# A two-phase mixer layer: adaLN columns loaded and summed together, an 18-strip first projection, later v, and another layout at the seam

## The chip, the core and the metric

The kernel runs on one core of one Trainium2 chip. Five engines work side by side, each through its own queue in order: TensorE (PE in the profile, with its weight loads as PEld), VectorE (DVE), ScalarE (ACT), GpSimd (POOL) and SyncE (SP), which here issues most of the DMA transfers. The metric is the device time of one execution in microseconds (us), as the median of several runs; it was 2493.97 us before (2492.70 to 2501.88 in 3 runs).

## What is computed

One layer of a hybrid model on a sequence of 2048 tokens of width 1024, all in float32: a mixer (a gated short convolution beside a gated delta rule with 4 heads of 128, in chunks of 64 tokens), a feed-forward part, and a last norm. Norms are adaptive: their shift and scale come from a condition vector c.

```python
def adaln(x, gain, shift, scale):
    return rms_norm(x, gain) * (1 + scale[:, None, :]) + shift[:, None, :]

mod = silu(c) @ w_ada + b_ada                      # 6 x 1024 columns
shift_m, scale_m, gate_m, shift_f, scale_f, gate_f = split(mod, 6)
h = adaln(x, g_norm_mix, shift_m, scale_m)
gate_b, gate_c, h_conv, q, k, v, z, a, bt = split(h @ w_in)
ya = group_norm(gate_b * conv3(gate_c * h_conv))
q, k, v = silu(conv4(concat(q, k, v)))
yb = rms_norm(chunked_gated_delta_rule(l2(q), l2(k), v, g(a), sigmoid(bt))) * silu(z)
x = x + gate_m * (concat(ya, yb) @ w_out)
h = adaln(x, g_norm_ffn, shift_f, scale_f)
gt, up = split(h @ w_gate_up)
x = x + gate_f * ((silu(gt) * up) @ w_down)
out = adaln(x, g_norm_final, shift_o, scale_o)
```

## The kernel before

The sequence is cut into four blocks of 512 tokens. A float32 product is made of three passes over rounded operands (high x high, high x low, low x high); `split_w` (L383 to L388) makes the high half of a weight strip on ACT (L385) and the low half on DVE (L387), or on the engine that `lo_engines` names.

**Opening and first phase.** Blocks 0 and 1 are projected together, by a fast scheme with seven products for each pair of strips (`PAIRS`), whose operands are sums of halves of the two blocks (A11, A12, S1 to S4, A22). Its first operands need x of block 0, normed and transposed, and the scale and shift columns of adaLN, `Gm` and `Sm`. These columns are sums over the 1024 rows of `w_ada`, in three parts of 3, 3 and 2 column groups of 128 (`PARTS`). For part 0, `sums_pe` (L842) sums the scale on PE with the condition column as the moving operand, and `sums_on` (L850) the shift on DVE. For parts 1 and 2 (`late`, `more_rows`, L1058) the scale is summed by DVE and the shift by ACT (multiply) and POOL (add). A sum over DVE or POOL is then added across partitions by PE (`col_sums`, L478). Each transfer is 128 rows of one half's columns, and all of them go round through sixteen places in four tiles, `kd`, `vt`, `zs` and `S3l` (`ada_slots`, L815). All are issued by SP, in the order of the program: x of block 0, the columns, the first four weight strips, the columns of parts 1 and 2, then the small constants, x of block 1 and further strips. `later_sums` (L1099) then norms, transposes and scales block 1 and builds S1 to S4 (L1109 to L1112), and splits them into halves (L1123, L1124). In this opening the framework's scheduler sets the order on each engine.

**Second phase.** From `early.close()` on, the order on each engine is set by a planner (`Clock`): it gives each instruction a cost and a time, places steps of chains between dense matmuls when their inputs are due, and pins that order. Four stages follow (`STAGES`, L410), one for each block whose delta rule is computed. Stage b projects some strips of block 2 or 3 (`dense_strip`, one strip of 128 columns of `w_in` is 24 matmuls), then computes `output(b)`, which multiplies the block's ya and yb with `w_out`. The order of strips is k, q, v, z (four each), then gc, hc, gb four times. While strips run, block b's chains run as side work: the decay, Gram matrices, an inverse of the triangular matrices step by step on DVE (L1449, L1451) with a turn through DRAM, the levels of the inverse (L1490 to L1533), v by `v_chain` (a load, a transposition on PE at L1335, a product at L1578), then the chunk chain (L1600 to L1629) and its outputs `ym` (L1654), which `output` waits for. A chain says how long after its inputs' planned end it wants its next step: `yield v, sk` stands for 0.3 us. `cv` is a tile with four buffers, for convolution, v and the output. Dense strips and outputs take their PSUM banks from one pool of four (`dense_ps`), chains from another of four (`misc_ps`).

**The seam.** After output 3 the mixer's tiles are given up and the feed-forward part begins (`first_sums`, `prep_weights`, `run`). Its pool `fp` starts at the same address as the mixer's pool `la`, which holds only the four `cv` tiles. A tile in the new pool waits for the old tiles under it. `prep_weights` builds its first tile there, `T`, at L1883.

Of the kernel before, what the change touches and what calls it, by code (L numbers as in the profile page):

```python
# [12 lines left out]
F32 = mybir.dt.float32  # L13
# [7 lines left out]
P = 128  # L21
# [189 lines left out]
def layer_kernel(ctx, tc, x, c, w_ada, b_ada, w_ada_final, b_ada_final, g_norm_mix, g_norm_ffn, g_norm_final,  # L211
# [198 lines left out]
    STAGES = (2, 0, 14), (2, 14, 28), (3, 0, 12), (3, 12, 28)  # L410
# [356 lines left out]
    with ExitStack() as actx:  # L767
# [31 lines left out]
        raw_a, raw_d, raw_s1 = (rb.tile([P, 4, BLK], F32, name=n) for n in ("A22h", "A22l", "S4h"))  # L799
        raw_c = rb.tile([P, 4, BLK], F32, name="S4l")  # L800
# [14 lines left out]
        def ada_slots():  # L815
            while True:
                for p, n in ((ra, "kd"), (ra, "vt"), (ra, "zs"), (rb, "S3l")):
                    t = p.tile([P, 4, BLK], F32, name=n)
                    for i in range(4):
                        yield t[:, i]  # L820
        slots = ada_slots()

        PARTS = range(3), range(3, 6), range(6, KD)

        def ada_raw(c0, ks):
            c0, n = c0 + ks[0] * P, len(ks) * P
            for k in range(KD):
                raw = next(slots)[:, :n]
                nc.sync.dma_start(raw, w_ada[k * P:(k + 1) * P, c0:c0 + n])
                yield k, raw  # L830
# [11 lines left out]
        def sums_pe(c0, ks):  # L842
            ps, n = misc_ps(), len(ks)
            for k, raw in ada_raw(c0, ks):
                for j in range(n):
                    mm(ps[:, j:j + 1], raw[:, j * P:(j + 1) * P], cs[:, k:k + 1], start=k + j == 0,
                       stop=k == KD - 1, skip_group_check=True)
            return ps[:, :n]

        def sums_on(eng, raws):  # L850
            acc = cv_tile([P, BLK])[:, :raws[0][1].shape[1]]
            for k, raw in raws:
                if eng is nc.gpsimd:
                    nc.scalar.activation(raw if k else acc, raw, AF.Identity, scale=cs[:, k:k + 1])
                    if k:
                        eng.tensor_add(acc, acc, raw)
                elif k == 0:
                    eng.tensor_scalar_mul(acc, raw, cs[:, 0:1])
                else:
                    eng.scalar_tensor_tensor(acc, raw, cs[:, k:k + 1], acc, op0=ALU.mult, op1=ALU.add)  # L860
            return acc
# [29 lines left out]
        ada_scale(sums_pe(D, PARTS[0]), PARTS[0])  # L891
        x_load(0, 2)
        x_load(0, 3)
        x_norm(0)
        sums = sums_on(nc.vector, list(ada_raw(0, PARTS[0])))
        raws = {p: [load_strip(PAIRS[p][0])] for p in range(EARLY)}
        late = {(c0, n): list(ada_raw(c0, PARTS[n])) for n in (1, 2) for c0 in (D, 0)}
# [4 lines left out]
        ada_shift(col_sums(sums, len(PARTS[0])), PARTS[0])  # L902
# [6 lines left out]
        lo_engines.extend([nc.vector, nc.vector, nc.gpsimd, nc.gpsimd])  # L909
# [187 lines left out]
        nc.scalar.copy(gones_r, gones)  # L1097

# [225 lines left out]
        def start_block(b, prev):  # L1324
# [240 lines left out]
            def v_chain(hs):  # L1565
                while "sk" not in done:
                    yield POLL
                yield from wait("mx", 1)
                if not B.vt:
                    B.vt.append(tile_of([P, CH, NH, P], "vt"))  # L1570
                for h in hs:
                    yield from take("cv", 1)
                    v = cv_tile([P, BLK])
                    nc.sync.dma_start(v, vd[b][h])
                    yield v, sk
                    pv = to_tokens(v)
                    give("cv", 1)
                    nc.vector.tensor_mul(B.vt[0][:, :, h, :], h4(pv), bc(sk[:, h], P))  # L1578
                    done["vt"] += 1
# [142 lines left out]
        def project(w=None):  # L1722
            ps = dense_ps()
            proj(ps, next_w(), *hT)
            return ps
# [103 lines left out]
        for b, (src, s0, s1) in enumerate(STAGES):  # L1829
# [4 lines left out]
            for s in STRIPS[s0:s1]:  # L1834
                dense_strip(src, s, B)
# [16 lines left out]
    fp = fctx.enter_context(tc.tile_pool(name="fp", bufs=1, side="left", reuse_waits="tile"))  # L1852
# [63 lines left out]
    def pair_sums(hf, i, acts):  # L1916
# [487 lines left out]
```

## Time and profile before

| | us |
|---|---|
| median of 3 runs | 2493.97 |
| the profiled execution | 2499.41 |
| its span, first to last instruction | 2497.6 |
| PE busy | 2344.1 |
| DVE busy | 1788.2 |
| ACT busy | 1140.8 |
| POOL busy | 621.3 |

The page gives, for one profiled execution, each engine's busy time, the span in 40 slices, the chain of work that ended last, and groups of instructions by line. Further views of the same trace are used below: PE's waits by what ended them, single instructions in order of time, and the busy time by stretches. In a timeline row the first number is the start in us from the beginning of the span, the second the duration; "x4" says that four were merged, and a bracket names the idle time before the row and what ended it. PE is busy 94% of the span; its granted clock, 1.00 when full, is 0.971 in the mean.

### The profile page before, as it was taken

The numbers are of one execution on the slowest core, as the hardware profiler recorded it, in microseconds if no ns is written. First come the engines' busy times: TensorE is split into PE (matmuls) and PEld (weight loads), VectorE is DVE, ScalarE is ACT, GpSimd is POOL, SyncE is SP. The second block draws the span as 40 slices with busy tenths as digits, with TensorE's granted clock in tenths as the row PEclk, the third lists the DMA queues.
The fourth block names the chain that finished last, engine by engine and source line by source line (L and its number), as shares of the span: only waits on it lengthen the run. The fifth ranks groups of instructions, "written<-read, shape, count | busy, mean of one in ns | idle before, by whom it ended". The sixth has DMA issues, their size and how long they took to land.

```text
span 2497.6 us, 31277 instructions
## 1 busy us (share of the span) xinstructions
PE 2344.1 (94%) x11149; PEld 1933.7 (77%) x11149; DVE 1788.2 (72%) x2699; ACT 1140.8 (46%) x1999; POOL 621.3 (25%) x711
## 2 busy tenths in 40 slices
PE   6899999778999898999999999999999999999997
PEld 5677777667887687887787888878888887887786
DVE  4866988857667697567568655786556569878887
ACT  5756567433653754455643333533333323322345
POOL 3322335144144044211000000000000026344447
PEclk8899999889999899999999999999999999999999
DMA  7736665425454543546477433574333356333334
GB/s 254 233 106 194 186 200 165 134 71 122 127 190 100 167 154 72 126 127 184 137 226 233 134 101 114 173 205 126 100 111 103 103 162 228 121 109 122 138 114 155
DMA packets 399830, 370.05 MB, mean 148 GB/s; under 512 B 41253, under 2 KB 326190, under 8 KB 399418
## 3 DMA queue, kind: packets, MB, share of 16 engines
q1 hardware_dynamic: 390058, 350.91, 45.7%
q0 software_dynamic: 4608, 8.39, 2.3%
q10 hardware_dynamic: 5008, 8.76, 0.9%
q8 instruction: 87, 1.43, 0.2%
q14 instruction: 69, 0.57, 0.1%
HBM read 271.51 MB, written 104.87 MB: 151 GB/s over the span
## 4 chain that ended last, share of the span: by engine, by line
PE 56%; DVE 10%; DMA 8%; issue 8%; POOL 4%; ACT 4%; SPq 0%; ACTq 0%; DVEq 0%; POOLq 0%
PE pd L318 33%; PE pm L318 16%; DVE acc L2258 1%; DMA cv<-v 1%; DVE wlo L387 1%; DMA x<-cv 1%; DMA y<-in_w_ada_final_dram 1%; DMA wraw<-in_w_gate_up_dram 1%; DVE y L467 1%; PE pm L1335 1%; POOL wraw L2187 1%; PE pm L1504 1%; POOL x L1823 1%; PE pm L1496 1%; PE pm L1600 0%
## 5 line engine op out<-in xcount | busy, mean ns | idle before, releaser
L385 ACT CAST whi<-wraw 128x1024 fp32r<-128x1024 f32 x264 | 276.4, 1049 | 348.2 <-PE pd L318 163.9
L387 DVE TENSOR_TENSOR wlo<-wraw,whi 128x1024 fp32r<-128x1024 f32 x262 | 322.8, 1233 | 72.9 <-ACT whi L385 71.7
L318 PE MATMUL pd<-r,whi 128*128 128x512 f32 x1008 | 350.0, 410 | 13.2 <-DVE r L1124 8.3
L318 PEld LDWEIGHTS pd<-r,whi 128*128 128x128 f32 x1008 | 194.5, 193 | 55.2 <-DVE r L1124 10.1
L318 PE MATMUL pd<-r,wlo 128*128 128x512 f32 x504 | 200.8, 398 | 0.0
L2060 POOL TENSOR_TENSOR ht<-y,ht 128x512 fp32r<-128x512 f32 x1 | 1.8, 1838 | 714.1 <-DVE wraw L1885 714.1
L2258 DVE TENSOR_TENSOR acc<-acc,pd 128x512 f32<-128x512 f32 x192 | 127.3, 679 | 25.8 <-PE pd L318 25.0
L2138 ACT CAST xh<-ra 128x640 fp32r<-128x640 f32 (+1 forms) x85 | 60.4, 722 | 183.4 <-PE pm L318 133.8
L2000 DVE TENSOR_TENSOR sg<-sg,pd 128x512 f32<-128x512 f32 x44 | 30.2, 686 | 158.2 <-PE pd L318 158.1
L318 PEld LDWEIGHTS pd<-r,wlo 128*128 128x128 f32 x504 | 97.7, 194 | 16.4
L318 PE MATMUL pd<-whi,ym 128*128 128x512 f32 x256 | 85.3, 406 | 15.8 <-ACT ym L1654 13.9
L2147 POOL TENSOR_TENSOR xl<-ra,xh 128x640 fp32r<-128x640 f32 (+1 forms) x37 | 62.2, 1680 | 146.1 <-ACT xh L2138 135.2
L318 PE MATMUL pd<-A22h,whi 128*128 128x512 f32 x232 | 91.3, 394 | 6.5 <-DVE u L1039 4.0
L2258 DVE TENSOR_TENSOR acc<-acc,pm 128x512 f32<-128x512 f32 x120 | 81.7, 681 | 18.4 <-PE pm L318 17.9
L318 PE MATMUL pd<-S3l,t3h 128*128 128x512 f32 x232 | 91.3, 393 | 0.0
L318 PE MATMUL pd<-A22l,whi 128*128 128x512 f32 x232 | 90.7, 391 | 0.0
L318 PE MATMUL pm<-S4h,whi 128*128 128x512 f32 x232 | 90.6, 390 | 0.2 <-ACT u L1036 0.2
L318 PE MATMUL pm<-S4l,whi 128*128 128x512 f32 x232 | 90.7, 391 | 0.0
L318 PE MATMUL pd<-A22h,wlo 128*128 128x512 f32 x232 | 90.6, 390 | 0.0
L318 PE MATMUL pm<-S4h,wlo 128*128 128x512 f32 x232 | 90.4, 390 | 0.0
L2187 POOL TENSOR_TENSOR wraw<-wraw 128x512 f32<-128x512 f32 x40 | 70.2, 1777 | 48.8 <-DMA wraw<-in_w_down_dram 42.6
L318 PE MATMUL pd<-S2h,whi 128*128 128x512 f32 x176 | 69.6, 395 | 11.9 <-ACT whi L385 11.1
(539 smaller groups left out, 6803.6 us busy)
## 6 DMA issues: line engine op xcount, KB each, us to landing
wraw<-in_w_gate_up_dram SPq DMA_DIRECT2D x88, 512.0 KB, 4.1
wraw<-in_w_in_dram SPq DMA_DIRECT2D x86, 512.0 KB, 5.0
ra<-act SPq DMA_DIRECT2D x80, 448.0 KB, 3.7
act<-S SPq DMA_DIRECT2D x80, 256.0 KB, 3.5
act<-act SPq DMA_DIRECT2D x68, 256.0 KB, 2.2
y<-in_w_ada_dram SPq DMA_DIRECT2D x32, 512.0 KB, 4.5
wraw<-in_w_out_dram SPq DMA_DIRECT2D x32, 512.0 KB, 5.0
wraw<-in_w_down_dram SPq DMA_DIRECT2D x22, 512.0 KB, 3.6
```

What stands on the lines that cost most here:

```text
L318: mm(*args, **kw)
L385: nc.scalar.copy(hi, raw)
L387: (lo_engines.popleft() if lo_engines else nc.vector).tensor_sub(lo, raw, hi.bitcast(F32))
L467: nc.vector.scalar_tensor_tensor(acc, raw, cs[:, k:k + 1], acc, op0=ALU.mult, op1=ALU.add)
L1335: nc.tensor.transpose(ps[:, j * P:(j + 1) * P], src[:, j * P:(j + 1) * P], ident)
L1496: mm(py[:, j * P:(j + 1) * P], Mm[h][:, j, :], T[h][:, j, :], start=True, stop=True)
L1504: mm(pz[:, j * P:(j + 1) * P], Y[h][:, j, :], Xs[h][:, j, :], start=True, stop=True)
L2000: nc.vector.tensor_add(s5[i], s5[i], a[i])
L2138: nc.scalar.copy(hi, raw[:, c0:c1, :])
L2147: eng.tensor_sub(lo, raw, hi.bitcast(F32))
L2187: nc.gpsimd.tensor_mul(r[:, hs], r[:, hs], gate_f[:, hs])
L2258: nc.vector.tensor_add(accs[s, u][:, ns], accs[s, u][:, ns], ps)
```

## The change

It has six edits:

- The first stage projects 18 strips of block 2 in place of 14, the second 10 in place of 14. The cut now falls between hc and gb of the first group.
- Each transfer of adaLN columns brings the shift and the scale columns of 128 rows together (8 transfers a part in place of 16). The parts have places of their own: part 0 in `kd`, `vt`, `zs`, `S3l`; part 1 in `S4h`, `S4l`, `kd`, `vt`; part 2 in `zs`, `S3l`. The tiles `raw_s1` and `raw_c`, which have the places `S4h` and `S4l`, are taken later.
- For part 0, PE sums the scale and DVE the shift as the transfers come; x's third and fourth chunk are loaded behind the fourth transfer. For parts 1 and 2, DVE sums both at once. Nothing of this is left on ACT and POOL, and the first four strips' low halves are all made by DVE.
- `v_chain` places its transposition 3.0 us after the planned landing of v, in place of 0.3.
- The first strip of each stage but the first takes its bank from `misc_ps`.
- The `S` tiles of the feed-forward part lie in a pool of their own, `fs`, ahead of `fp`.

```diff
-    STAGES = (2, 0, 14), (2, 14, 28), (3, 0, 12), (3, 12, 28)
+    STAGES = (2, 0, 18), (2, 18, 28), (3, 0, 12), (3, 12, 28)
...
-        raw_a, raw_d, raw_s1 = (rb.tile([P, 4, BLK], F32, name=n) for n in ("A22h", "A22l", "S4h"))
-        raw_c = rb.tile([P, 4, BLK], F32, name="S4l")
+        raw_a, raw_d = (rb.tile([P, 4, BLK], F32, name=n) for n in ("A22h", "A22l"))
...
+        PLACES = (((ra, "kd"), (ra, "vt"), (ra, "zs"), (rb, "S3l")), ((rb, "S4h"), (rb, "S4l"), (ra, "kd"), (ra, "vt")),
+                  ((ra, "zs"), (rb, "S3l")))
+
+        def ada_raw(part):
+            ks, n_t = PARTS[part], KD // len(PLACES[part])
+            c0, n = ks[0] * P, len(ks) * P
+            rows = w_ada[:, 0:2 * D].rearrange("k (s c) -> k s c", s=2)
+            for q, (pool_, name) in enumerate(PLACES[part]):
+                t = pool_.tile([P, n_t, 2, n], F32, name=name)
+                for i in range(n_t):
+                    k = q * n_t + i
+                    nc.sync.dma_start(t[:, i], rows[k * P:(k + 1) * P, :, c0:c0 + n])
+                    yield k, t[:, i]
...
+        def sums_first():
+            ps, acc, n = misc_ps(), cv_tile([P, BLK])[:, :len(PARTS[0]) * P], len(PARTS[0])
+            for k, raw in ada_raw(0):
                 for j in range(n):
-                    mm(ps[:, j:j + 1], raw[:, j * P:(j + 1) * P], cs[:, k:k + 1], start=k + j == 0,
+                    mm(ps[:, j:j + 1], raw[:, 1, j * P:(j + 1) * P], cs[:, k:k + 1], start=k + j == 0,
                        stop=k == KD - 1, skip_group_check=True)
+                if k == 0:
+                    nc.vector.tensor_scalar_mul(acc, raw[:, 0], cs[:, 0:1])
+                else:
+                    nc.vector.scalar_tensor_tensor(acc, raw[:, 0], cs[:, k:k + 1], acc, op0=ALU.mult, op1=ALU.add)
+                if k == 3:
+                    x_load(0, 2)
+                    x_load(0, 3)
+            return ps[:, :n], acc
+
+        def sums_both(raws):
+            n = raws[0][1].shape[2]
+            acc = temp()[:, :2 * n].rearrange("p (s c) -> p s c", s=2)
             for k, raw in raws:
-                if eng is nc.gpsimd:
-                    nc.scalar.activation(raw if k else acc, raw, AF.Identity, scale=cs[:, k:k + 1])
-                    if k:
-                        eng.tensor_add(acc, acc, raw)
-                elif k == 0:
-                    eng.tensor_scalar_mul(acc, raw, cs[:, 0:1])
+                if k == 0:
+                    nc.vector.tensor_scalar_mul(acc, raw, cs[:, 0:1])
                 else:
-                    eng.scalar_tensor_tensor(acc, raw, cs[:, k:k + 1], acc, op0=ALU.mult, op1=ALU.add)
+                    nc.vector.scalar_tensor_tensor(acc, raw, cs[:, k:k + 1], acc, op0=ALU.mult, op1=ALU.add)
             return acc
...
-        ada_scale(sums_pe(D, PARTS[0]), PARTS[0])
-        x_load(0, 2)
-        x_load(0, 3)
+        ps_g, acc_s = sums_first()
         x_norm(0)
-        sums = sums_on(nc.vector, list(ada_raw(0, PARTS[0])))
         raws = {p: [load_strip(PAIRS[p][0])] for p in range(EARLY)}
-        late = {(c0, n): list(ada_raw(c0, PARTS[n])) for n in (1, 2) for c0 in (D, 0)}
+        late = {n: list(ada_raw(n)) for n in (1, 2)}
...
+        ada_scale(ps_g, PARTS[0])
+        ada_shift(col_sums(acc_s, len(PARTS[0])), PARTS[0])
...
-        lo_engines.extend([nc.vector, nc.vector, nc.gpsimd, nc.gpsimd])
...
-            g, sh = (sums_on(e, late.pop((c0, n))) for e, c0 in ((nc.vector, D), (nc.gpsimd, 0)))
+            acc = sums_both(late.pop(n))
             yield
             n_k = len(PARTS[n])
-            ada_scale(col_sums(g, n_k), PARTS[n])
-            ada_shift(col_sums(sh, n_k), PARTS[n])
+            ada_scale(col_sums(acc[:, 1], n_k), PARTS[n])
+            ada_shift(col_sums(acc[:, 0], n_k), PARTS[n])
...
+        raw_s1, raw_c = (rb.tile([P, 4, BLK], F32, name=n) for n in ("S4h", "S4l"))
...
-                    yield v, sk
+                    yield 3.0, v, sk
...
-        def dense_strip(b, s, B):
+        def dense_strip(b, s, B, bank=dense_ps):
...
-            ps = project()
+            ps = project(bank())
...
-                dense_strip(src, s, B)
+                dense_strip(src, s, B, misc_ps if b and s == STRIPS[s0] else dense_ps)
...
-    fp = fctx.enter_context(tc.tile_pool(name="fp", bufs=1, side="left", reuse_waits="tile"))
+    fs, fp = (fctx.enter_context(tc.tile_pool(name=n, bufs=1, side="left", reuse_waits="tile")) for n in ("fs", "fp"))
...
-            t[o] = fp.tile([P, BLK], F32, name="S", bufs=4)
+            t[o] = fs.tile([P, BLK], F32, name="S", bufs=4)
```

More of the change, by code (lines that the diff above doesn't have):

```diff
@@ L813, in x_norm @@
                     nc.scalar.activation(xts[b][i - 1], xts[b][i - 1], AF.Identity, scale=ss[i - 1])
[L815 to L821, printed above, removed]
-        PARTS = range(3), range(3, 6), range(6, KD)
[L825 to L830, printed above, removed]
+        PARTS = range(3), range(3, 6), range(6, KD)
+        PLACES = (((ra, "kd"), (ra, "vt"), (ra, "zs"), (rb, "S3l")), ((rb, "S4h"), (rb, "S4l"), (ra, "kd"), (ra, "vt")),
[10 more added lines that the diff above has]
+                    yield k, t[:, i]
         def ada_scale(sums, ks):
@@ L901, in layer_kernel @@
             nc.scalar.copy(to[:, k4, :], turned(0, k))
-        ada_shift(col_sums(sums, len(PARTS[0])), PARTS[0])
+        ada_scale(ps_g, PARTS[0])
+        ada_shift(col_sums(acc_s, len(PARTS[0])), PARTS[0])
         H["A11"] = [ra.tile([P, 4, BLK], F32R, name="kq", bufs=2) for _ in range(2)]
@@ L1720, in layer_kernel, with project @@
                 halos[3] = tile_of([P, 12, 3], "halo1"), tile_of([P, 4, 2], "uhalo1")
-        def project(w=None):
-            ps = dense_ps()
+        def project(ps):
             proj(ps, next_w(), *hT)
```

6 lines of the change are left out of this document (removed).

## The prediction

> **What bounds the kernel now.** I read the page first, then the list of PE's waits, then the busy time by stage.
>
> ```profile
> span 2497.6 us, 31277 instructions
> ...
> PE   6899999778999898999999999999999999999997
> ...
> PEclk8899999889999899999999999999999999999999
> ```
>
> Each digit is the busy share of a fortieth of the span (62.4 us), the second row is the granted clock. From slice 20 (1249 us) on PE is full but for the last, so what this change can move lies before: the opening (slices 0 and 1), the delta-rule blocks (slices 6 to 18) and the seam to the feed-forward part behind them, too short to show here.
>
> ```profile
> PE pm L1335 <- DMA cv<-v: 21.4, 9, 4.5
> PE pd L318 <- ACT ym L1654: 13.9, 5, 4.7
> PE pd L318 <- DVE r L1124: 8.3, 3, 5.5
> ```
>
> PE's waits (sum, times, longest): the loads of v, the outputs of the chunk chain, and in the opening the split of S2.
>
> ```profile
> 0.00:28.00 28.00, 17.36 (x88) 16.59 (x88) 6.98 (x17) 15.80 (x26) 4.49 (x16) 1.00 0.95 312
> 28.00:58.00 30.00, 21.90 (x71) 17.16 (x72) 21.91 (x26) 17.64 (x32) 18.81 (x17) 0.72 0.60 190
> 58.00:99.00 41.00, 27.13 (x115) 18.51 (x113) 31.42 (x59) 33.28 (x59) 15.42 (x22) 0.77 0.83 280
> ...
> 475.00:606.00 131.00, 99.52 (x617) 85.24 (x615) 85.88 (x211) 42.03 (x145) 52.29 (x76) 0.88 0.33 91
> 606.00:740.00 134.00, 122.68 (x720) 104.70 (x721) 87.79 (x128) 69.15 (x134) 38.53 (x60) 0.94 0.54 155
> 740.00:804.00 64.00, 62.15 (x314) 50.51 (x314) 51.39 (x122) 29.20 (x84) 27.91 (x32) 0.97 0.47 116
> ```
>
> Columns: stretch, length, busy PE, weight loads, DVE, ACT, POOL, granted clock, DMA share, GB/s. Output of block 0 (475 to 606) leaves PE idle 31.5 us; output of block 1 (740 to 804) leaves 1.9. The opening idles 8.1 (28 to 58) and 13.9 us (58 to 99), at clocks of 0.72 and 0.77: where PE waits, what it does next also runs slower.
>
> **A, the opening.** Before, the scale columns are summed first by PE, the shift columns by DVE; for parts 1 and 2 by DVE and by ACT with POOL. All parts use the same four places, so loads wait for sums. After, each transfer brings both halves (8 per part instead of 16, same bytes), and part 1 lies half in places not used before.
>
> ```profile
> 21.48 2.58 DVE L860 SCALAR_TENSOR_TENSOR cv<-S3l,cs,cv 128x384 f32<-128x384 f32 x4
> ...
> 23.25 2.06 ACT L901 COPY A22l<-pm 128x512 f32<-128x512 f32 x4
> ...
> 28.36 3.12 SPq L829 DMA_DIRECT2D S3l<-in_w_ada_dram  x4
> ...
> 29.39 1.22 PE L318 MATMUL pd<-kq,whi 128*128 128x512 f32 x2 [4.37 <-ACT whi L385]
> ...
> 34.83 5.22 DVE L860 SCALAR_TENSOR_TENSOR cv<-kd,cs,cv 128x384 f32<-128x384 f32 x3
> ...
> 40.07 1.75 SPq L829 DMA_DIRECT2D kd<-in_w_ada_dram  x4
> ...
> 41.00 4.98 POOL L856 TENSOR_TENSOR cv<-cv,S3l 128x384 f32<-128x384 f32 x4
> ...
> 45.28 2.31 PE L481 MATMUL pm<-ones_r,cv 128*128 128x16 f32 x12 [4.36 <-DVE cv L860]
> ...
> 48.75 1.53 DVE L860 SCALAR_TENSOR_TENSOR cv<-vt,cs,cv 128x256 f32<-128x256 f32 x3
> ...
> 51.23 2.29 SPq L805 DMA_DIRECT2D r<-in_x_dram  x4
> ...
> 75.19 0.68 DVE L1109 TENSOR_TENSOR S4h<-S4l,y 128x512 f32<-128x512 f32 x1
> ```
>
> ```profile
> L387 DVE TENSOR_TENSOR wlo<-wraw,whi 128x1024 fp32r<-128x1024 f32 x262 | 322.8, 1233 | 72.9 <-ACT whi L385 71.7
> ```
>
> Timeline rows give start and duration; the last row is a group of the page (busy, mean ns of one). *Part 0*: the scale sum now needs 1.5 MB more to land (5 us at the 312 GB/s of the first row above), the shift sum follows the loads instead of starting behind the scale. No gain: ACT copies until 25.3 us and the first product at 29.39 waits for ACT. *Part 1*: a DVE sum of 384 columns takes 0.645 us alone (2.58/4), but 1.74 (5.22/3) while POOL works. A 768-column one isn't in the trace; between 0.645 and 1.29, I take 1.05, by the step from 256 (0.51) to 384. Eight make about 8 us, two wlo splits taken from POOL add 2.5, the seven slowed sums drop; DVE's total stays about where it was, the sums end near 38 instead of just before 45.28, and PE's first products run until 40.9 (45.28 - 4.36). The wait of 4.36 goes; late next is the scaling by ACT. *Part 2 and the queue*: SP stands from 31.5 to 40.07 and holds every later load. After, nothing waits there: part 2 and then x of block 1 are issued some 15 us sooner. What is loaded up to and with x (2 MB of x, 3.1 for part 0, 2.1 of strips, 3.1 and 2.1 for parts 1 and 2, 2.1 of x) is 14.5 MB, which at 312 GB/s lands near 48 us, so the norm, the transposes and the sums that start with the row at 75.19 come about 10 us earlier, when DVE still has gaps. Of the idle 22 us from 28 to 99, I take **half, -11**; ends -4 (only the wait before L481) and -17 (three quarters). Held at nothing: the later allocation of S4h and S4l (their first other use is behind these sums).
>
> [...]
>
> **B, 18 strips first.** Four strips (z2, z3, gc0, hc0) go ahead of output 0.
>
> ```profile
> 1247.87 5.44 PE pd L318 x24
> ```
>
> A strip is 24 matmuls, 5.44 us by this row of the chain of waits; four are 21.8.
>
> ```profile
> 501.46 2.49 DVE L1490 STREAM_TRANSPOSE lv<-X 128x512 f32<-128x512 f32 x4
> ...
> 502.32 5.81 PE L1496 MATMUL pm<-lv,ym 128*128 128x128 f32 x32 [15.02 <-DVE lv L1490]
> ...
> 559.42 0.59 ACT L1654 CAST ym<-pm 128x512 fp32r<-128x512 f32 x1 [2.08 <-DVE pm L1650]
> ...
> 624.80 2.49 DVE L1490 STREAM_TRANSPOSE lv<-X 128x512 f32<-128x512 f32 x4
> ...
> 723.08 0.59 ACT L1654 CAST ym<-pm 128x512 fp32r<-128x512 f32 x1 [3.48 <-DVE pm L1650]
> ```
>
> Output 0 needs its chain, which ends with the last ym at 560; before it PE idles 15.02 us at once, now covered by these strips. The chain runs on DVE, and four splits (4 x 1.23) and hc0's convolution (about 2.5) are queued among its steps: it ends 0 to 14 us later, I take **+5**. Stage 1 has 21.8 us less to do and loses its v stalls; but output 1 then meets its own chain. By the trace its last ym comes at 723.7, and of the 64 us of output 1 only 42 matmuls (9.5 us) go ahead of it: 723.7 + 54.5 = 778, 26 before 804. If the chain itself advances as PE stalls less, up to 34. I take **-29**. B together **-24** (ends -12 and -34). The cv buffer that hc0 holds over output 0 leaves three of four; I cost it at nothing, since the four evictions of a half are spread over some 9 us of PE work; where they come at once DVE stands behind the store.
>
> **C, later v.** The transposes of v are placed 3.0 instead of 0.3 us after the planned landing.
>
> ```profile
> 814.90 1.09 PE L1335 MATMUL pm<-ck,cv 128*128 128x128 f32 x4 [4.50 <-DMA cv<-v]
> ...
> 824.47 0.66 PE L1335 MATMUL pm<-ck,cv 128*128 128x128 f32 x4 [1.97 <-DMA cv<-v]
> ...
> 1008.93 1.97 PE L1335 MATMUL pm<-ck,cv 128*128 128x128 f32 x8 [3.44 <-DMA cv<-v]
> ...
> 629.65 1.28 DVE L1578 TENSOR_TENSOR vt<-pm,sk 128x512 f32<-128x512 f32 x2
> ...
> 651.85 1.82 DVE L1533 TENSOR_SCALAR X<-pm 64x256 f32<-64x256 f32 x4 [3.95 <-PE pm L1531]
> ```
>
> Blocks 0 and 1 are in B. In blocks 2 and 3 the waits are 9.9; shortened by 2.7 each, 2.5 stay, so **-7** (ends -2 and -12, with the slow clock behind them). Who waits for v: the chunk chain, which also needs the inverse; in block 1 v ends at 630.9, the inverse at 653.7, so a later v is covered by 22 us.
>
> **D, the bank.** The first strip of a stage takes a misc bank, not one that output still empties.
>
> ```profile
> 608.30 0.70 PE L318 MATMUL pd<-r,whi 128*128 128x512 f32 x2 [2.34 <-DVE cv L1822]
> ...
> 998.18 0.70 PE L318 MATMUL pd<-r,whi 128*128 128x512 f32 x2 [2.02 <-DVE cv L1822]
> ```
>
> **-4** (0 to -7). The third stage begins with the narrow product in a misc bank already.
>
> **E, the seam.** The S tiles, used late, get the addresses of the cv tiles; before, T lay there.
>
> ```profile
> 1178.49 0.69 DVE L1884 TENSOR_TENSOR wraw<-wraw 128x512 f32<-128x512 f32 x1
> ...
> 1188.02 0.69 DVE L1883 TENSOR_TENSOR T<-wraw 128x512 f32<-128x512 f32 x1 [8.84 <-DMA x<-cv]
> ...
> 1192.30 0.80 PE L318 MATMUL pd<-S2h,whi 128*128 128x512 f32 x1 [11.05 <-ACT whi L385]
> ```
>
> T waits for the last stores out of cv, and PE for what follows T, 4.28 us later. Without that T starts at 1179.1 and PE at 1183.4: **-9** (-5 to -11). Under T lie the mixer's small tiles then, whose chains have ended; late next is the cast of the strip on ACT, which is in the 4.28.
>
> **The sum**: -11 - 24 - 7 - 4 - 9 = -55. The profiled execution took 2499.41 us (span 2497.6), so 2444; the median of the runs is 2493.97, 5.4 lower, and 2494 - 55 gives 2439. I say 2440.
>
> **Rivals.**
> 1. *Output 1 waits in place of output 0.* For it: the last ym of block 1 comes 98 us after its transposes, in block 0, with PE idle, only 58. If block 0 slows by 20 and block 1 doesn't advance, B is +20 - 26 = -6: 2494 - 37 = 2457. Against: PE was not once late for ym in stage 1.
> 2. *The opening becomes DVE-bound*: DVE is busy 31.4 of the 41 us from 58 to 99. A is 0: 2450.
> 3. *Slower: the chains set all ends.* Block 0 runs at the interleaved pace (98 instead of 58, +40), and the later blocks, also chain-bound, return nothing of B, C and D: +40 - 11 - 9 = +20, 2514. It decides if, between the row at 501.46 and the last ym, dense strips stand ahead of most chain steps. Against: in stages 1 and 2 PE waited little for ym (4.7 at most).
> 4. *The change doesn't do what it says*: the opening's scheduler or the planner orders the work in another way and the waits come back elsewhere; within 12 us of 2494.
>
> **How the numbers follow.** Forecast 0.70 (2424 to 2462 by itself), rival 1 0.12, rival 2 0.08, rival 3 0.05, rival 4 0.05. All lower ends together make 2494 - 81 = 2413, all upper ones 2494 - 23 = 2471; both unlikely at once, so 2420 below; above I go past them to 2476, for part of rivals 3 and 4. About 0.5% is what a measurement of this kernel can tell from no change (2481.5 to 2506.4): faster 0.90, same 0.05, slower 0.05.
>
> **What would show it.** A: no stop of SP from 31.5 to 40, L481 without its wait, L1109 near 65. B: the 15 us wait before L1496 gone, last ym of block 0 near 565, a wait of output 1 for ym below 8 us. C: waits for v below 3 us in all. D: no wait for L1822 at a stage's start. E: T within 2 us of L1884. Wrong it goes above all where a chain step is queued behind dense work on PE or DVE: then ym is late in both outputs.

## The result, and the profile after

The changed kernel takes 2473.57 us (median of 4 runs, 2471.34 to 2477.91) against 2497.93 beside it: ratio 0.9905, 95% interval 0.9875 to 0.9934. That is some 24 us, where 55 were forecast. Its profiled execution took 2473.61 us, with this page:

```profile
span 2471.7 us, 31212 instructions
...
PE   6899999989798799899999999999999999999998
...
PEclk9899999999799799999999999999999999999999
```

Against before, PE's slices 7 to 9 (433 to 618 us, 61.8 each) have risen from 7, 7, 8 to 9, 8, 9: the output of block 0 is filled. But slices 10, 12 and 13 (618 to 680 and 742 to 865 us) have fallen from 9, 9, 8 to 7, 8, 7. The list of PE's waits (engine, line, what ended the wait: sum, times, longest) says why:

```profile
PE pm L1683 <- ACT lv L1678: 19.6, 3, 9.0
PE pm L1496 <- DVE lv L1490: 14.5, 4, 11.6
...
PE pd L318 <- ACT ym L1654: 8.0, 4, 2.6
PE pd L318 <- DVE r L1124: 7.9, 3, 5.5
...
PE pm L1335 <- DMA cv<-v: 4.5, 3, 3.1
```

The waits for v have gone from 21.4 to 4.5 us, those for ym from 13.9 to 8.0, nearly as forecast (v below 3 in all). But 34 us of others stand at the top: for the mix chain (L1683) and the level chain (L1496). Before, L1683 had none, and L1496 hardly more than the one of 15.02 us in output 0, which is gone. The table of busy time by stage follows. A stage runs from the end of one stage's last output product to the end of the next one's; the columns are those of the prediction. First come stages 1 and 2 before, then stages 0 to 2 after:

```profile
606.00:800.30 194.30, 181.14 (x1017) 153.55 (x1018) 135.79 (x238) 97.30 (x217) 66.00 (x91) 0.95 0.52 145
800.30:996.20 195.90, 178.96 (x994) 149.92 (x992) 146.32 (x282) 107.25 (x232) 67.01 (x91) 0.94 0.47 131
```

```profile
475.00:606.40 131.40, 117.00 (x711) 100.19 (x712) 93.43 (x220) 47.57 (x152) 52.56 (x76) 0.97 0.39 109
606.40:784.60 178.20, 160.63 (x921) 138.74 (x920) 124.82 (x220) 87.82 (x206) 67.96 (x91) 0.92 0.53 144
784.60:983.70 199.10, 174.42 (x995) 147.98 (x994) 148.23 (x290) 97.50 (x225) 64.61 (x91) 0.91 0.47 131
```

Stage 0 now holds 94 matmuls more between 475 us and its end, and ends where it did. Stage 1 has 20.5 us less of PE work (181.14 to 160.63), but its idle time *rose*, from 13.2 to 17.6 us. Stage 2 is 3.2 us longer at nearly the same count of matmuls: 24.7 us idle instead of 16.9.

PE's timeline at the start of stage 2 (start, duration, instruction, in brackets the idle time before it and what ended that):

```profile
793.41 0.39 PE L318 MATMUL pm<-r,wlo 128*128 128x512 f32 x1
795.78 0.60 PE L1145 MATMUL pm<-ck,cv 16*128 16x16 f32 x4 [1.98 <-DVE cv L1141]
802.77 0.58 PE L1683 MATMUL pm<-lv,gones_r 128*128 128x256 f32 x1 [6.39 <-ACT lv L1678]
...
808.41 1.12 PE L598 MATMUL pm<-ck,wraw 128*128 128x128 f32 x4 [1.34 <-ACT cv L1686]
821.08 6.41 PE L1496 MATMUL pm<-lv,ym 128*128 128x128 f32 x32 [11.55 <-DVE lv L1490]
...
839.89 0.95 PE L318 MATMUL pd<-r,whi 128*128 128x512 f32 x2
```

Between 793.8 and 839.9 PE runs no dense product at all: one strip is done, and then only chain steps, the longest of them waited for. I call this a *dense-free stretch*. In stage 1 there is one of 42.7 us, from 617.2. Before, the longest in these two stages were 9.3 and 8.3 us; the one of stage 1 runs from 615.6 to 624.9:

```profile
618.29 0.66 PE L1335 MATMUL pm<-ck,cv 128*128 128x128 f32 x4 [2.67 <-DMA cv<-v]
...
624.91 0.78 PE L318 MATMUL pd<-r,whi 128*128 128x512 f32 x1
```

A wait on a chain step costs PE its whole length where no dense work stands beside it, and here none does.

That the cv buffers are short shows already at the end of output 0. Its last four results on DVE, before and then after:

```profile
607.47 2.48 DVE L1822 TENSOR_TENSOR cv<-pd,gate_m 128x512 f32<-128x512 f32 x4
...
613.18 0.69 DVE L1821 TENSOR_TENSOR cv<-pd,gate_m 128x512 f32<-128x512 f32 x1 [3.45 <-DMA x<-cv]
```

Before, the four follow each other. After, the strip hc0 keeps one of the four buffers over the output, and the fourth result waits 3.45 us for a store out of cv to end.

The seam, DVE's rows and then PE's (line numbers are those of the changed kernel, here one lower than before):

```profile
1165.85 0.69 DVE L1883 TENSOR_TENSOR wraw<-wraw 128x512 f32<-128x512 f32 x1
1166.45 1.30 DVE L1882 TENSOR_TENSOR T<-wraw 128x512 f32<-128x512 f32 x2
...
1169.48 0.50 PE L318 MATMUL pd<-S2h,whi 128*128 128x512 f32 x1 [0.88 <-ACT whi L385]
```

T follows its neighbour at once, and PE starts S2 6.5 us after stage 3's end (1163.0), where it took 16.7 before.

The opening, by DVE's, SP's and PE's rows:

```profile
33.09 3.17 SPq L804 DMA_DIRECT2D r<-in_x_dram  x4
...
36.59 0.62 DVE L859 TENSOR_SCALAR y<-S4h,cs 128x768 f32<-128x768 f32 x1
37.24 1.02 DVE L861 SCALAR_TENSOR_TENSOR y<-S4h,cs,y 128x768 f32<-128x768 f32 x1
...
43.84 1.01 DVE L861 SCALAR_TENSOR_TENSOR y<-vt,cs,y 128x768 f32<-128x768 f32 x1
...
45.00 1.48 PE L481 MATMUL pm<-ones_r,y 128*128 128x16 f32 x12 [1.77 <-DVE y L861]
...
74.22 0.68 DVE L1109 TENSOR_TENSOR S4h<-S4l,y 128x512 f32<-128x512 f32 x1
```

SP no longer stands: x of the second half is issued at 33.09 instead of 51.23. A sum of 768 columns takes 1.02 us, as estimated (1.05). Yet part 1's sums only begin at 36.59 and end at 44.85, the wait before L481 is 1.77 us where none was forecast, and L1109 comes at 74.22, one us earlier than before and not near 65.

### The profile page after: what moved, and what is told of

It is laid out like the page before. It is cut to its first block, busy times and chain, and to the rows that moved or that the text cites. A ratio compares the mean times of both kernels' runs of the same rounds, so it can differ in the third digit from the quotient of the medians.

```text
span 2471.7 us, 31212 instructions
## 1 busy us (share of the span) xinstructions
PE 2336.1 (95%) x11149; PEld 1930.6 (78%) x11149; DVE 1783.7 (72%) x2701; ACT 1121.2 (45%) x1973; POOL 598.7 (24%) x695
## 4 chain that ended last, share of the span: by engine, by line
PE 43%; DVE 6%; DMA 4%; ACT 2%; issue 2%; POOL 1%; DVEq 0%; SPq 0%; POOLq 0%; ACTq 0%
PE pd L318 25%; PE pm L318 16%; DVE acc L2257 1%; DMA y<-in_w_ada_final_dram 1%; DVE xl L2146 0%; POOL acc L2271 0%; ACT whi L385 0%; DVE y L467 0%; DMA y<-xT 0%; DVE dl L2178 0%; DMA y<-in_w_ada_dram 0%; POOL wraw L2186 0%; DMA ra<-act 0%; PE pm L598 0%; DVE wlo L2178 0%
## 5 line engine op out<-in xcount | busy, mean ns | idle before, releaser
L318 PE MATMUL pd<-r,whi 128*128 128x512 f32 x960 | 327.1, 405 | 8.5 <-DVE r L1124 7.9
L318 PEld LDWEIGHTS pd<-r,whi 128*128 128x128 f32 x960 | 183.1, 191 | 47.0 <-DVE r L1124 10.1
L318 PE MATMUL pd<-r,wlo 128*128 128x512 f32 x480 | 189.6, 395 | 0.6 <-DVE wlo L387 0.6
L318 PEld LDWEIGHTS pd<-r,wlo 128*128 128x128 f32 x480 | 91.9, 192 | 16.7 <-DVE wlo L387 1.0
L1305 DVE SCALAR_TENSOR_TENSOR cv<-pd,pcb,cv 128x511 f32<-128x511 f32 (+2 forms) x85 | 63.6, 748 | 14.7 <-ACT cv L1303 12.5
```

The lines of the kernel that those rows point to most:

```text
L318: mm(*args, **kw)
L1305: nc.vector.scalar_tensor_tensor(cv[:, n - t:], u[:, :BLK - n + t], taps[t], cv[:, n - t:], op0=ALU.mult, op1=ALU.add)
```

## The experiments

Three theories on the stages. **Theory 1**: chain steps are placed too early, because their loads land late behind the output's accumulating stores. **Theory 2**, formed after the first runs: the four cv buffers run out. A dense strip of these stages needs one or two for its convolution (`take_now` places chain steps alone until one comes free), a v chain holds one, a mix chain two, the rates one. **Rival**: the chains set the ends, and dense products only trade places with waits. (In the expectation of `cv_5_buffers` theory 2 is still called rival 2; in those of `price_3_no_c` and `null_before` rival 2 is something else, that every edit of the planner re-deals the order.) Each ratio is to runs of the kernel before on the same chip; stage lengths are taken as above, from the one profiled execution of each kernel.

**C alone undone** (`c_undone`).

```diff
-                    yield 3.0, v, sk
+                    yield v, sk
```

> The changed kernel with the v chain due at its usual 0.3 us again instead of 3.0; all else as changed. Theory 1 (a later v hands its wait to the next chain step, because every step of the chains behind the output's accumulating stores is planned too early): the time is within 4 us of the changed kernel's 2473.6 (2470 to 2478), the waits before the v transposes are back (10 us and more in stages 1 and 2 together) and the waits before L1683 and L1496 (33 us in all in the changed kernel's stages 1 and 2) are shorter by about as much. Rival (the forecast's term, a v that is not waited for shortens blocks 2 and 3 by 7 us by itself): about 2481, and the waits before L1683 and L1496 stay as long as they are.

Measured: 2465.26 us, 0.9886 (0.9859 to 0.9914). The waits before the v transposes are back (5.6 us in stage 1 and 5.3 in stage 2; the profile puts the second down to DVE), and those before L1683 and L1496 in these stages fell from 33 to 5 us. Stage 0 ends 7.9 us later (614.3), stage 2 takes 190.5 instead of 199.1, stage 3 177.4. Both readings missed: by the ratios the later v as a whole costs about 5 us, which is not to be told from zero (10 either way). The dense-free stretches fell to 21.5 and 10.4 us; yet stage 1 is as long as in the change (177.5 and 178.2), so the length of such a stretch alone does not measure the loss.

**B and C undone** (`bc_undone`): also `STAGES = (2, 0, 14), (2, 14, 28), ...`.

> The changed kernel with the stages cut at 14 strips and v due at its usual time again: what is left of the change is the opening, the bank and the seam. Theory 1 (of the 18 strips only the stages' own difference, 3.8 us lost in stage 0 and 16 won in stage 1, is worth anything, and the later v is worth about nothing): 2473.6 + 12 = about 2485, range 2480 to 2490. Rival (the forecast's sizes for the two terms, 24 and 7 us, are right and the opening, the bank or the seam cost what is missing): 2473.6 + 31 = about 2504.

Measured: 2479.13 us, 0.9948 (0.9929 to 0.9966): 0.43% above the change, 11 us (9 either way), as theory 1 has it (the time is just below its range), and not 31. So opening, bank and seam together give 0.5%, some 13 us, and B (this run against the last) 0.6%, some 15. Stage 0 ends at 603.7, stage 1 takes 193.9, stage 2 188.7.

**A dearer store in the planner** (`pool_price_3`; `price_3_no_c` with C undone too).

```diff
             begin = self.fit([eng], start, 0.45) - 0.45
+            if "Pool" in eng:
+                cost *= 3.0
```

> The changed kernel with one figure of its planner altered: a store on the GpSimd queue is priced at three times its bytes (a 256 KB store 2.1 us of the DMA engines instead of 0.69; four of them occupy the engines for some 10 us in the trace), so loads behind the stores are expected later and chain steps that wait for them are put behind more dense products. The instructions are the same, their order differs. Theory 1 (the planner's too low price puts the steps too early, and dense work is there to fill the wait): the waits before L1683 and L1496 in stages 1 and 2 fall from 33 us to under 17, and the time by 8 to 20 us, to 2454 to 2466. Rival (the chain itself sets the end of these stages, dense products only trade places with the wait): the time stays within 5 us of 2473.6 and waits of about the same sum stand later in the stages.

> The changed kernel with the GpSimd queue's stores priced at three times their bytes and the v chain due at its usual 0.3 us: both edits that helped by themselves. Theory 1 (both take away the same thing, steps planned too early behind the stores): stage 2 takes 188 to 192 us as without the later v (199.1 as changed), the waits before L1683 at the stages' starts stay at the 5 us that the price left, and the time is 2460 to 2466, at or under that without the later v alone. Rival (the gains are of different waits and add): 2473.6 less 8 less 4 = 2461 or less, stage 0 as short as with the price (602.1 us at its end). Rival 2 (stage lengths answer to each edit of the planner by some us in no order): stages 0 to 2 differ from both parents by 4 us and more in either direction, the time anywhere in 2458 to 2476.

Measured: 2469.52 us, 0.9914 (0.9887 to 0.9941), and 2468.92, 0.9905 (0.9876 to 0.9933). In the first, the waits named fell to 23 us, not under 17, stage 1's dense-free stretch stayed at 41.6 us while stage 2's broke into two of 14.7 and 16.0, and the time is not to be told from the change's. The second isn't faster than C undone alone, and its stage 2 (193.8) is above the 188 to 192 expected. Theory 1 doesn't carry the loss.

**Five cv buffers** (`cv_5_buffers`; `cv_5_no_c` with C undone too): `NCV, NLV, NCHN = 5, 6, 4`, and the pad tile beside them cut from 536 to 4 columns.

> The changed kernel with five buffers of the name cv instead of four (the room comes from a pad tile). Rival 2 (with the cut at 18 strips a gate strip keeps one cv over output 0, and it is the missing buffer that holds up the mix chain's load at the start of stage 1): the load L1672 is issued by 612 us instead of 617, the 9.0 us wait before L1683 at 617 to 626 us falls under 3, and the time by 6 to 10 us, to 2464 to 2468. Theory 1 (the load lands behind the four accumulating stores, which keep the 16 DMA engines busy until about 618, whenever it is issued): the wait before L1683 stays over 5 us and the time within 4 us of 2473.6.

> The changed kernel with five cv buffers and v due at its usual time. Theory 2 (the four cv buffers run out): stage 1 is 3 to 6 us shorter than with four (177.5), stage 2 2 to 5 us shorter (190.5), and the waits at their starts under 10 us together; stage 0's first part may be some 9 us longer, as with five buffers before (the mix chains of block 0 then wait among its strips); the time 2456 to 2465. Theory 1 (late landings): stages 1 and 2 within 2 us of 177.5 and 190.5.

Measured: 2471.9 us, 0.9913 (0.9887 to 0.9938), and 2476.66, 0.9934 (0.9909 to 0.9959). Stage 1 falls to 172.9 and, without C, to 167.2, more than theory 2 asked for; stage 2 is 195.5 and 193.2, the second a miss. In the first, the four results of output 0 follow each other again, and the first mix load of stage 1 goes out 6.3 us after stage 0's end instead of 10.8, so that the wait before L1683 falls from 9.0 to 3.7 (under 3 was expected). But dense-free stretches of 34.0 and 29.8 us remain: with the late v, one more buffer does not end them. Neither kernel gains as a whole: in both, stage 0 ends 5 to 8 us later, with waits of some 7 us for mix chains among its strips near 400, and in the second the seam waits 9.7 us again for the split of S2.

**A planner edit that means nothing** (`null_before`): the usual lateness 0.32 instead of 0.3, on the kernel before.

> The kernel before with every step's usual lateness in the planner 0.32 us instead of 0.30: an edit that means nothing for any wait of the trace (0.02 us a step). If the planner answers smoothly, every stage ends within 1 us of before (606.0, 800.3, 996.2, 1175.8) and the time within 2 us. If a small shift re-deals the order of chain steps and products (rival 2), stages change by 3 us and more, as stage 2 did between 188.7 and 199.1 in kernels that do not differ there, and the time by up to 8 us in either direction.

Measured: 2494.66 us, 1.0004 (0.9988 to 1.0019). Single stages moved by up to 4.5 us (stage 0 ended at 601.5) and paid it back. So a stage length of one trace is taken here as good to some 4 us, and the time holds.

**The opening, part 1 first** (`part1_ahead`; `part1_and_norm_ahead`).

```diff
-        raws = {p: [load_strip(PAIRS[p][0])] for p in range(EARLY)}
-        late = {n: list(ada_raw(n)) for n in (1, 2)}
+        raws = {p: [load_strip(PAIRS[p][0])] for p in range(2)}
+        late = {1: list(ada_raw(1))}
+        raws.update({p: [load_strip(PAIRS[p][0])] for p in range(2, EARLY)})
+        late[2] = list(ada_raw(2))
...
         Ws, x0 = {}, {}
+        acc1 = sums_both(late.pop(1))
...
+        x_norm(1)
         for _ in gens[1]:
```

The last added line, with `x_norm(1)` taken out of `later_sums`, is in the second alone.

> The changed kernel with the loads of part 1's columns ahead of the second two strips of weights, and part 1's sums written ahead of the four weight splits, instead of behind both. Theory (the sums ended at 44.85 instead of 38 because DVE was given the four splits first): the eight sums end by 40 us, the 1.77 us wait before L481 at 45 us goes, but the first L1109 stays within 2 us of 74.2, because the second half's norms set it, and the opening's end (374.1 us at stage 0's first dense strip) within 2 us; the time within 4 us of 2473.6. Rival (the forecast: earlier sums move the whole opening): the opening ends 4 us earlier or more.

> As the run before, and the norm of the second half of x written ahead of part 1's rows instead of in the later sums: ACT was idle from 34.8 to 46.8 us and x's second half had landed by 42.6, yet its squares and scales ran from 53.9 to 67.7. Theory (order, not data, holds the second half back): the first L1109 moves from 74.2 to 70 or earlier and the 5.55 us wait before the products at 87.5 us shrinks by 3 or more; the opening's end comes 2 to 5 us earlier. Rival (the 8 norm instructions, 12 us of ACT, now stand ahead of part 1's and 2's rows, and the products wait for those instead): the first L1109 moves, but the waits before 60 us grow by as much and the opening's end stays within 1 us.

Measured: 2469.68 us, 0.9903 (0.9872 to 0.9934), and 2469.31, 0.9905 (0.9875 to 0.9934): no gain over the change. The sums end at 40.6 us, the wait before L481 falls to 0.81, and what is L1109 in the change comes earlier: in the first by 3.4 us, where at most 2 were expected, in the second by 7.1. But the opening's end, the first product of stage 0's first dense strip, stays: 374.06 us in the change, 374.99 and 374.86 here. In the second that is the rival's reading.

```profile
70.84 0.68 DVE L1112 TENSOR_TENSOR S4h<-S4l,y 128x512 f32<-128x512 f32 x1
```

```profile
67.12 1.73 DVE L1112 TENSOR_TENSOR S4h<-S4l,y 128x512 f32<-128x512 f32 x1
```

In the second, DVE then is full: its window shows 31.48 of 32 us busy, where the change has 27.84:

```profile
66.00:98.00 32.00, 25.49 (x100) 16.78 (x98) 31.48 (x56) 25.52 (x45) 14.09 (x11) 0.81 0.65 222
```

**The opening undone** (`opening_undone`): the kernel before with B, C, D and E.

> The kernel before with B, C, D and E of the change, the opening as before. Theory (the new opening is worth what its trace shows, 3 us): 2473.6 + 3, range 2473 to 2481. Rival (the forecast's 11 us are there, and another part costs what is missing): 2485.

Measured: 2468.48 us, 0.9899 (0.9874 to 0.9925), below both readings. By the ratios the new opening costs 1.5 us (10 either way), and its end is 375.10 here against 374.06: it is worth nothing that can be told from zero, and not 11 us.

**A late v in block 0 alone** (`late_v_block0`).

```diff
-                    yield 3.0, v, sk
+                    yield 3.0 if b == 0 else 0.3, v, sk
```

> The changed kernel with v's lateness of 3.0 us kept for block 0 alone, 0.3 for blocks 1 to 3. By the stages of the runs so far a later v is worth 6 us in stage 0 (109.4 against 115.3 us from the first output product to the last), nothing in stage 1, and costs 8.6 in stage 2 (199.1 against 190.5) and 2 in stage 3. Theory 1 (these are effects of the late v, each in its own block): stage 0's output takes 109 to 111, stage 2 takes 190 to 192, and the time is 6 us under that without the later v (2465.3): 2457 to 2462. Rival (the planner's order is re-dealt by every edit and the stage lengths belong to no block): stage lengths off by 4 us and more from this table, the time anywhere in 2460 to 2475.

Measured: 2458.21 us, 0.9858 (0.9843 to 0.9872), by the ratios 12 us (8 either way) faster than the change: this is what the later v costs in blocks 1 to 3. Stage 0's output 109.4, stage 2 190.4, stage 3 176.6, as theory 1 of this run has it: each block answers to its own v.

**Mix chains behind v** (`mix_after_v`, with C undone; `cv_5_mix_after_v` with five buffers and the late v of block 0).

```diff
             def mix_chains():
+                yield from wait("vt", NH)
                 for m in range(4):
```

> The changed kernel with v due at its usual time and one more wait in the code's order: a block's mix chains begin when its four v tiles are turned, so that the mix chain (two cv buffers) and the two v chains (one each) no longer hold all four cv buffers at once. Theory 2 (PE waits on chain steps at the start of stages 1 and 2 because the next dense strip can't be placed: its convolution needs a cv buffer, the chains hold all four, and the code then places chain steps alone until one comes free): dense products run again between the chain steps, no 15 us stretch of stage 1 or 2 is without one, the waits before L1683, L1335 and L1496 in both fall from 18 us to under 8, and the time to 2450 to 2459. Theory 1 (the steps wait for loads that land late): the v loads still land late, their waits stay, and the time is within 4 us of 2465. Rival: the mix chain, begun later, is late for the output's last products (a wait before L318 for yah over 5 us): 2465 or more.

> Five cv buffers, the mix chains behind the v tiles, and v's lateness of 3.0 us in block 0 alone. Theory 2 (buffers): stages 1 and 2 as in the run with the mix chains behind v alone, since four buffers then do, within 2 us; stage 0's output 109 to 111 us; 2446 to 2456. Theory 1: no shorter than 2459.

Measured: 2489.67 us, 0.9983 (0.9971 to 0.9996), and 2490.89, 0.999 (0.9979 to 1.0002): misses as times. But stage 1 fell to 163.8 and 165.8 us, without any dense-free stretch over 8 us. With `c_undone` (177.5) and `cv_5_no_c` (167.2) these make a square: the fifth buffer shortens stage 1 by 10 us where the mix chains come first and not at all where they come behind v. So in stage 1, as far as one trace of each can tell, it is the buffers that the early mix chain takes away. The loss is elsewhere: in the first, stage 0 ends 6.5 us later than with C alone undone (620.8), stage 2 takes 212.0, and its output waits, by its timeline:

```profile
927.13 0.80 PE L318 MATMUL pd<-whi,ym 128*128 128x512 f32 x1 [4.54 <-ACT ym L1654]
...
950.34 0.80 PE L318 MATMUL pd<-whi,ym 128*128 128x512 f32 x1 [7.86 <-ACT ym L1654]
```

There the dense strips ran ahead of the chains, and the output paid 12.4 us of waits for ym: in that stage the rival of the three theories is right, though not by the wait for yah that the expectation named.

**Only where it pays** (`mix_late_block1`; `mix_late_blocks12`, behind two v tiles instead of four; both with the late v of block 0 alone).

```diff
             def mix_chains():
+                if b in (1, 2):
+                    yield from wait("vt", 2)
                 for m in range(4):
```

The first has `b == 1` and `NH` here.

> The changed kernel with v's lateness in block 0 alone (2458.2) and, in block 1 alone, the mix chains behind the four v tiles. Theory 2 (in stage 1 the chains hold all four cv buffers and the dense strips stand still for it): stage 1 takes 164 to 168 us instead of 178.4, stages 0, 2 and 3 stay within 3 us of 109.4, 190.4 and 176.6, and the time is 2444 to 2451. Rival (the work moved ahead in stage 1 is paid back in the next stage, as with the mix chains late in all blocks, since stage 2 starts with its chains less far): stage 1 falls as above, stage 2 grows by 8 or more, and the time is 2454 to 2462.

> As before, but in blocks 1 and 2, and behind the first two v tiles instead of all four, so that the mix chain is held up less. Theory 2: stages 1 and 2 each 5 us shorter or more than 178.4 and 190.4, time under 2450. Rival (the chains set the end of stage 2, so that dense strips placed earlier only make the output wait for its inputs): stage 2 is no shorter than 190 and its output has waits before L318 for ym or ya of 8 us and more.

Measured: 2463.1 us, 0.9887 (0.9868 to 0.9906), and **2446.39 us, 0.9818 (0.9798 to 0.9837)**, the fastest of all: 10 us (6 either way) below `late_v_block0`. In the first, stage 1 takes 163.9 us and stage 2 205.5: the rival's bill. In the second:

```profile
606.30:772.20 165.90, 156.48 (x921) 133.19 (x921) 122.91 (x212) 86.52 (x206) 68.10 (x91) 0.97 0.55 154
772.20:966.70 194.50, 176.72 (x996) 147.87 (x994) 153.60 (x298) 103.42 (x230) 66.51 (x91) 0.94 0.47 132
```

Stage 1 idles 9.4 us instead of 17.6 with the same 921 matmuls, at a clock of 0.97 instead of 0.92. Stage 2 came out 4 us longer than in `late_v_block0`, against theory 2, though no more than one trace can tell; its output waits only 1.5 us for ym, against the rival. Why stage 2 is not shorter stays open. It still has one wait of 11.0 us, for a v load issued at 793.44. The dense-free stretches are 11.4 and 11.7 us.

SP's issues into cv buffers at the start of stage 2, before, after, and in this kernel, show the order in which the chains get them:

```profile
807.79 3.54 SPq L1574 DMA_DIRECT2D cv<-v  x2
819.27 1.02 SPq L1574 DMA_DIRECT2D cv<-v  x2
820.39 0.39 SPq L1672 DMA_DIRECT2D cv<-ya  x1
847.41 0.32 SPq L1672 DMA_DIRECT2D cv<-ya  x1
```

```profile
793.16 0.34 SPq L1672 DMA_DIRECT2D cv<-ya  x1
799.53 0.53 SPq L1574 DMA_DIRECT2D cv<-v  x1
814.50 0.45 SPq L1672 DMA_DIRECT2D cv<-ya  x1
814.99 0.43 SPq L1574 DMA_DIRECT2D cv<-v  x1
819.86 0.32 SPq L1672 DMA_DIRECT2D cv<-ya  x1
842.58 0.32 SPq L1574 DMA_DIRECT2D cv<-v  x1
```

```profile
793.44 1.02 SPq L1574 DMA_DIRECT2D cv<-v  x2
797.78 2.59 SPq L1574 DMA_DIRECT2D cv<-v  x2
804.81 0.53 SPq L1672 DMA_DIRECT2D cv<-ya  x1
823.57 0.67 SPq L1672 DMA_DIRECT2D cv<-ya  x1
```

Before, four v in pairs and then one mix tile at a time. After, a mix tile comes first and takes two of the four buffers, the v tiles follow singly, and the third is issued at 842.58, after the dense strips have begun again (the fourth at 852.22). Holding the mix chain behind two v tiles gives the old order back.

## Why the prediction was wrong, and where it was right

By the ratios the shares are: opening, bank and seam 13 us (24 forecast), B 15 (24), C about -5 (+7). With differences between two runs uncertain by 0.3 to 0.4%, B and C are good to some 8 to 10 us, and the first sum to 5. Single traces give the same signs with other sizes: at the end of stage 3, `c_undone` is 6.5 us ahead of `bc_undone` and 3.5 ahead of the change.

- **A, -11: wrong, about 0.** The step that failed is "the sums end near 38" (they end at 44.85), and behind it "the norm, the transposes and the sums [...] come about 10 us earlier" (L1109 came one us earlier). The queue was freed as forecast, but DVE had been given all four weight splits ahead of the sums, and ACT ran the second half's squares from 53.9 us though x had been issued at 33.09. Undoing these orders moved L1109 by 3 and 7 us and the opening's end not at all: with both undone DVE has no gap left, as in rival 2, and what lead the change has by 142 us is partly given back at a lower clock (below). Rival 2 has the right size, nothing.
- **B, stage 0 +5: right in its mechanism** (0 in the change, with C; 10.5 by `c_undone` against `bc_undone`, in the forecast's 0 to 14). The 15.02 us wait is covered, the last ym cast of block 0 comes at 559.96, and the output waits at most 2.6 us for ym (forecast: near 565, below 8). The stage ended 0.4 us later than before, with the later v; 8 later without it.
- **B, stage 1 -29: the mis-sized term; it measured -16** (194.3 to 178.2 us). The strips' 21.8 us came out (20.5), but "loses its v stalls" did not hold: the waits moved to the mix and level chains. The forecast priced each wait by the event that ended it and did not ask who holds the buffers that let dense work run beside it. It looked at one cv buffer, hc0's, and said "I cost it at nothing": with it held, the fourth result of output 0 waits 3.45 us. At the start of stage 1, by the code's count, a mix chain (load at 617.18) and two v chains (618.58 and 620.43) then hold all four. With the mix chains behind two v tiles stage 1 takes 165.9 us, 28 less than before: the size was there to be had.
- **C, -7: wrong in sign.** The forecast put it in blocks 2 and 3; the later v of blocks 1 to 3 costs 12 us (8 either way, `late_v_block0` against the change). The step that failed is that a wait shortened by 2.7 us is worth 2.7 us. The waits for v did shrink (21.4 to 4.5), but stage 2 is 8.6 us longer with the late v, and stage 3 some 2, which one trace can't tell. A v that is turned later gives its buffer back later; that this is the means in stage 2 is argued from the code and from the order of the issues, the runs show the block and the price. In block 0, where the output itself runs at the pace of the chains, the later v shortens the output by 6 us and the time by 7 (8 either way, `late_v_block0` against `c_undone`).
- **D, -4: as forecast in the trace, not priced by a run.** The waits of 2.34 and 2.02 us at the starts of stages 1 and 3 are gone; in stage 1 the freed time leads into the chains' waits.
- **E, -9: right by the trace,** 10.2 us (16.7 to 6.5); no run undoes it alone.
- **Rivals.** Number 2 has what became of A. Number 4, "the waits come back elsewhere", named what happened in stages 1 and 2, with 0.05, but with a time within 12 us of 2494; the mechanism, the shared buffers, was in none.

## What to carry to other kernels

A wait for a chain costs little while other work can be issued beside it (stage 1, with the same 921 matmuls, idles 17.6 us in the change and 9.4 with the mix chains behind two v tiles): before pricing its removal, count the buffers that the chains and the bulk work share at that place, and who holds how many for how long. Placing one step later need not be free when it holds such a buffer, and the same edit may pay in one block and cost in the next: try it by block. When an edit brings half of what was forecast, look for the longest stretch without bulk work, not only for the longest wait; it shows where to look, not how much is lost.

## What the runs showed of the hardware

A wait of PE for 2 us can be followed by a stretch at half the clock, or not. The wait before L1184 is 2.08 us long and ends at 172.81 with the opening undone; in the change it is 2.03 us long and ends at 169.07. The windows of the first kernel and then of the second (the number after the busy times is the granted clock):

```profile
98.00:142.00 44.00, 43.75 (x184) 35.48 (x183) 33.57 (x51) 22.66 (x34) 12.08 (x11) 0.93 0.45 134
...
160.00:180.00 20.00, 17.92 (x91) 14.40 (x90) 9.23 (x27) 13.42 (x23) 5.11 (x8) 1.00 0.46 127
...
370.00:390.00 20.00, 18.67 (x96) 14.14 (x94) 13.68 (x18) 15.28 (x26) 12.84 (x12) 1.00 0.93 322
```

```profile
98.00:142.00 44.00, 44.00 (x197) 36.28 (x197) 35.79 (x48) 22.26 (x34) 11.80 (x11) 1.00 0.44 126
...
160.00:180.00 20.00, 17.97 (x82) 14.64 (x82) 8.47 (x26) 13.24 (x23) 5.63 (x10) 0.91 0.54 145
...
370.00:390.00 20.00, 16.56 (x66) 11.75 (x65) 10.27 (x9) 11.40 (x22) 14.75 (x21) 0.83 0.94 313
```

The new opening runs 13 matmuls more from 98 to 142 us and 9 fewer from 160 to 180, where its clock is 0.91: by an estimate from these figures 1.8 us are lost there (20 x 0.09), and 3.4 us from 370 to 390 (20 x 0.17). In windows of 1 us the clock of the change is 0.58 from 171 to 172, 0.50 for two more and 0.71 from 174 to 175, so half speed for some 3.4 us, from about 171.2 to 174.6. With part 1 ahead (wait of 2.05 us; 0.73 from 168 to 169, 0.50 for six more and 0.86 from 175 to 176) it is some 6.8 us, from about 168.5, and with the opening undone it stays at 1.00.

The wait before L1184 is 2.01 to 2.09 us long in all 17 profiled kernels, and from 160 to 180 us the clock falls below 1.00 in 8 of them. Kernels whose openings do not differ fall on both sides: the change has 0.91 after a wait that ends at 169.07, and `pool_price_3` has 1.00 after one of 2.01 us that ends at 169.12. So the wait and its place in the program do not decide it alone; these are single executions, and what does decide, and what sets the lengths of 3.4 and 6.8 us, was not measured. Nor does the prediction's "where PE waits, what it does next also runs slower" hold for every wait: before, the clock was 0.50 from 29 to 35 us, behind the wait of 4.37 us that ended at 29.39, and 1.00 from 160 to 180 around the wait of 2.02 us before L1184.
